# Pair loads and a narrower dense part in a PEER trunk kernel

## The chip, the cores and the metric

The kernel runs on one core of a Trainium2 chip. The metric is the device time of that core for one execution, in microseconds (us). Before the change it was 1577.41 us, the median of three runs (1571.57, 1577.41 and 1578.13).

## The reference, cut to what matters

Two layers act on 256 tokens of width 1024. Each layer mixes tokens (gated convolution, window attention and spatial gating) and then runs PEER: each token picks 16 of 16384 single-neuron experts in each of 8 heads.

```python
q = (t @ w_pq).reshape(T, PEER_HEADS, 2, PEER_HALF)
s = jnp.einsum('thpk,hpnk->thpn', q, sub_keys)
top_s, top_i = lax.top_k(s, PEER_TOPK)            # twice 16 of 128 keys per head
...                                               # best 16 of the 256 sums: experts, gate
u = expert_down[experts]                          # 128 rows of 4 KB for a token
act = gelu(einsum('td,thkd->thk', t, u))
vv = expert_up[experts]                           # 128 more rows
return einsum('thk,thkd->td', gate * act, vv)
```

`expert_down` and `expert_up` are tables of 16384 rows of 1024 float32 numbers, 64 MB each in each layer.

## The kernel before, in words

**Layer 0 and layer 1** have the same stages: mixing, retrieval (queries, key scores, the choice of experts) and experts. The change is about the experts stage, which has two parts of 128 steps each.

**The down part** multiplies the whole down table with the activations: step i takes chunk i of the table (128 experts, 512 KB, one tile `raw` of 128 partitions x 4 KB) and makes 8 products of 128x128 with the first T tokens (line 1233 of `experts`, by `chunk_mm` and line 359). The hidden values go to `acts`, by Gelu and then times a gate matrix that a small matmul makes for four tokens at a time (`gate_mm`, line 1135). **The up part** (`combine`) multiplies the chunks of the up table with `acts`, 8 products for a chunk (line 1173). TensorE is in order, so these chunks set its course.

**The other tokens**, the last S - T, take no part in the dense products, which are T columns wide (`DENSE`, 168 columns in layer 0 and 160 in layer 1). For each of them GpSimd gathers its 128 chosen rows (`fetch`, line 1076: one indirect transfer of 128 rows x 4 KB = 512 KB), first from the down table, where VectorE makes the products (`dot`, line 1086), then from the up table, where VectorE adds them up with weights (`add_row`, line 1101). The sums join the dense result by a few matmuls behind the last chunk (`folds`, line 1179). A gathered row set lies in one of some free places (`free`); a new gather starts when VectorE has used up a place. So layer 0 has 2 x 88 gathers and layer 1 has 2 x 96.

**The order of the loads** is one list, `seq`, for the whole program: conditioning weights, mixing weights and the chunks. Its tiles come from a ring of `RAW` = 7 tiles of 4 KB per partition. Even chunks are issued by ScalarE's queue ("second", line 258, with `QUEUE_LAG`), odd ones by SyncE's (line 217). Fifteen down chunks of a layer ("early") are loaded ahead to places in the arena that nothing else uses yet (`AHEAD_AT`), during mixing and retrieval. Conditioning weights for layer 1 ("aside", 512 KB each) come between the chunks on SyncE's queue; 40 of the 48 come during layer 0's experts stage, and 8 during layer 1's.

**When the gathers start and how fast they are used** follows numbers: `DOT_RATE` sets how many down rows VectorE takes per chunk, and line 1186 spreads the up rows evenly over the chunks from 4 to 124.

Of the kernel before, what the change touches and what calls it, by code (L numbers as in the profile page):

```python
# [9 lines left out]
F32 = mybir.dt.float32  # L10
# [7 lines left out]
P = 128  # L18
DEPTH = 2
S = 256  # L20
DC = 8
D = 1024
# [6 lines left out]

NP = 64  # L30
FRONT = 56
RAW = 7
AHEAD = 300
GROUPS = ("q0", "q1", "kv", "sv", "cc", "ch", "cb", "su")
IN_ORDER = ('q0', 'q1', 'kv', 'sv', 'cc', 'ch', 'cb', 'su')
# [5 lines left out]
PLAN1 = ((5, 'qk_sums k_norm'), (6, 'v_tok'), (7, 'lg10 exp'), (8, 'lg01 lg00 sm00'), (10, 'lg11'), (11, 'sm01 cz'), (12, 'sg'), (13, 'pt00 pt01 sm10 pv0'), (14, 'inv0 ao0 cy pt10'), (15, 'sm11 pt11 inv1 gs4 pv1 as0 ao1 gn4 mix'), (16, 'as1 an0'), (17, 'an1 sqrt'), (20, 'gs6 gn6'))  # L41
G_LAST = 124
OUT_AT = (3, 5, 6, 7)
DENSE = (168, 160)
QUEUE_LAG = 4
PICKS_LAG = 2
LOWER_LAG = 1
# [2 lines left out]
SETS_KNOWN = 22  # L50
D_FIRST = 8
DOT_SLOW = 0.3
DOT_RATE = (0.85, 0.92)
DOT_FAST = 1.6
RETIRE = 9
AHEAD_AT = (8, 12, 16, 36, 40, 44, 48, 52, 56, 60, 64, 68, 100, 28, 32)
KEPT = 100
FLUSH = 6
FIRST_LOWER = 1
AHEAD_FIRST = 4  # L60
# [21 lines left out]

@with_exitstack
def hybrid_trunk(ctx: ExitStack, tc: tile.TileContext, x_in, c_in, vec_in, w_ada, w_in, w_out, w_pq,
                 keys, down, down_rows, up, rel_bias, sgu_w, sgu_b, out):
    nc = tc.nc
    consts = ctx.enter_context(tc.tile_pool(name="consts", bufs=1))
    stream = ctx.enter_context(tc.tile_pool(name="stream", bufs=1))
# [44 lines left out]
    def region(at, *shape):  # L133
        n = 1
        for s in shape:
            n *= s
        v = flat[:, at:at + n]
        if len(shape) == 2:
            v = v.rearrange("p (a b) -> p a b", b=shape[1])
        elif len(shape) == 3:  # L140
            v = v.rearrange("p (a b c) -> p a b c", b=shape[1], c=shape[2])
        return v
# [51 lines left out]
    class Src:  # L194
        credit = 0.0
        loaded = 0
        cast = 0
        seq = []
        later = []
        aside = 0  # L200
# [5 lines left out]
    def dma_ahead(upto):  # L206
        while Src.loaded < min(upto, len(Src.seq)):
            kind, src, raw = Src.seq[Src.loaded]
            if kind == "aside":
                raw = stream.tile([P, D], F32, name="aside", tag=("hi", "lo")[Src.aside % 2], bufs=3)  # L210
                Src.aside += 1
            elif kind != "early":
                raw = stream.tile([P, D], F32, name="raw", tag="raw", bufs=RAW)
            if kind == "second":
                Src.later.append((Src.loaded, raw, src))
            else:
                nc.sync.dma_start(raw, src)
            raws[Src.loaded] = raw
            Src.loaded += 1
# [18 lines left out]
    def ada_end(layer, col, n):  # L238
        if (col + 1) % n == 0:
# [3 lines left out]
            if lo // 8 in (SC1 // 8, SC2 // 8):  # L243
                at = lo % 8 + (V_N1 if lo // 8 == SC1 // 8 else V_N2)
                nc.vector.scalar_tensor_tensor(m, m, 1.0, vec[:, layer, at:at + n], op0=OP.add, op1=OP.mult)

    def load_more(k):
        while Src.loaded < min([len(Src.seq)] + Src.limits) and (Src.ring[Src.loaded + 1] == Src.ring[Src.loaded]
                                             or Src.ring[Src.loaded] <= Src.ring[k + 1] + RAW - 2):
            dma_ahead(Src.loaded + 1)  # L250

    def cast_step(late=None):
        k = Src.cast
        if k >= len(Src.seq):
            return False
        dma_ahead(k + 1)
        while Src.later and Src.ring[Src.later[0][0]] <= Src.ring[k + 1] - 1 + RAW - QUEUE_LAG:
            nc.scalar.dma_start(*Src.later.pop(0)[1:])
        kind, _, arg = Src.seq[k]
        raw = raws.pop(k)  # L260
        Src.cast += 1
        if kind == "aside":
            Src.asides.append((k, lambda: ada_chunk(arg[0], arg[1], raw)))
        elif kind == "ada":
            ada_chunk(arg[0], arg[1], raw)
        elif kind in ("whole", "early", "second"):
            ready.append((raw, None))
        else:
            hi = stream.tile([P, D], F32R, name="hi", tag="hi", bufs=3)
            lo = stream.tile([P, D], F32R, name="lo", tag="lo", bufs=3)  # L270

            def low():
                if arg is None:
                    nc.vector.tensor_sub(lo, raw, hi.bitcast(F32))  # L274
                else:
                    nc.vector.scalar_tensor_tensor(lo, raw, arg, hi.bitcast(F32), op0=OP.mult,
                                                   op1=OP.subtract)

            with tc.high_priority(offset=AHEAD):
                if arg is None:  # L280
                    nc.scalar.copy(hi, raw)  # L281
                else:
                    nc.scalar.activation(hi, raw, AF.Copy, scale=arg)
                if late is None:
                    low()
                else:
                    late.append(low)
            ready.append((hi, lo))
        load_more(k)
        return True  # L290
# [27 lines left out]
    def mats(src, layer, n, kind="mat"):  # L318
        return [(kind, src[layer, p], None) for p in range(n)]

    seq = []
    for layer in range(DEPTH):
        body = [("whole" if n in WHOLE_IN[layer] else "mat", w_in[layer, n], None) for n in range(16)]
        tail = [("whole" if k in WHOLE_OUT[layer] else "mat", w_out[layer, k], vec[:, layer, V_OG + k:V_OG + k + 1])
                for k in OUT_ORDER[layer]]
        if layer == 0:
            first = []
            for d in range(DC):
                first += [("ada", w_ada[0, o + d], (0, o + d)) for o in (SC1, SH1)]
            head = [("early", b[1], region(at * S, 4, S).rearrange("p a b -> p (a b)"))  # L330
                    for b, at in zip(body, EARLY)]
            n = len(head)
            body = head + body[n:]
            body = first[:2] + body[:n] + first[2:] + mix(body[n:], ada(0, [2, 3, 4]))
        body += mix(tail[:6], ada(0, [5])) + tail[6:] if layer == 0 else tail
        seq += body + [("whole" if n in WHOLE_PQ else "mat", w_pq[layer, n], None) for n in range(16)]
        dn, un = ([t if n % 2 else ("second", *t[1:]) for n, t in enumerate(mats(w, layer, 128, "whole"))]
                  for w in (down, up))
        for n, at in enumerate(AHEAD_AT):
            dn[AHEAD_FIRST + n] = ("early", dn[AHEAD_FIRST + n][1], region(at * S, D))  # L340
        aside = ada(1, [0, 1, 2, 3, 4] if layer + 1 < DEPTH else [5], "aside")
        for n, at in reversed(tuple(enumerate(ASIDES_AT[layer]))):
            dn.insert(at, aside[n])
        if layer + 1 < DEPTH:
            un = mix(un, aside[len(ASIDES_AT[layer]):], *ASIDES_UP)
        Src.starts.append(len(seq))
        seq += dn + un
# [2 lines left out]
        Src.ring.append(Src.ring[-1] + was if Src.ring else 0)  # L350
        was = t[0] not in ("early", "aside")
    Src.ring.append(Src.ring[-1] + was)
    dma_ahead(RAW)

    def products(dst, w, cols, k, start, stop, **kw):

# [480 lines left out]
    def retrieval(layer, update, late):  # L837
# [132 lines left out]
        manual.close()  # L970
        for d in range(DC):
            nc.scalar.activation(R_HX[:, d, :], R_H[:, d, :], AF.Identity, bias=shifts[:, d:d + 1])
        Src.limits = [Src.starts[layer] + AHEAD_FIRST + n for n in (10, 13)]
        for pair in range(1, 8):
            if pair > 1:
                ps = bank("ch", 2)
# [33 lines left out]
    def experts(layer, rest):  # L1010
# [151 lines left out]
                a = acts[:, i:i + 2, :tdone]  # L1162
                nc.vector.tensor_mul(a, a, tmp[:, :, :tdone])

        rows = up.rearrange("l j i c -> (l j i) c")

        def combine(layer, late, dotted):
            qg = None
# [60 lines left out]
        for i in range(128):  # L1229
# [66 lines left out]
            n = i - AHEAD_FIRST  # L1296
# [136 lines left out]
```

## Time and profile before

| | |
|---|---|
| median of three runs | 1577.41 us |
| the profiled execution's own time | 1573.99 us |
| its span in the profile | 1572.1 us |
| TensorE busy | 1535.2 us (98%) |
| VectorE busy | 1000.1 us (64%) |
| ScalarE busy | 472.6 us (30%) |
| GpSimd busy | 494.8 us (31%) |
| moved by DMA | 571.21 MB, mean 363 GB/s |

From the times at which the first chunk products and the last ones stand in the trace, the stages of the profiled execution are: mixing and retrieval of layer 0 until 188 us, its down part until 507.5, its up part until 813.3; layer 1's mixing and retrieval until 973.5, its down part until 1283.5 and its up part until 1565.2. A busy TensorE is not a TensorE at its peak, since the ends of matmuls are modelled; how often its matmuls start says more. A row of waits tells which engine at which line waited, for what, how many us in total, how many times, and the longest time. The rows of a DMA view tell a queue's packets, its MB and the share of 16 DMA engines that its packets took; q1 is SyncE's queue, q10 ScalarE's and q0 GpSimd's.

### The profile page before, as it was taken

What the parts mean: (1) busy time and instruction counts of PE and PEld (TensorE: products, weight loads), DVE (VectorE), ACT (ScalarE), POOL (GpSimd) and SP (SyncE); (2) the same over time, 40 slices, a digit from 0 to 9 for tenths busy, and PEclk for the clock granted to TensorE, in tenths of its full rate; (3) what the DMA queues carried; (4) which work ended last, traced back from release to release, by engine and by line L of the source; (5) the groups of instructions that cost most, each with busy time, mean ns of one, the idle gap of its engine ahead of it and who ended that gap; (6) DMA issues with size and microseconds to landing.
All of it is one profiled execution on the core that took longest, in us unless ns stands there. A gap on an engine that the chain in (4) does not pass through costs nothing.

```text
span 1572.1 us, 28958 instructions
## 1 busy us (share of the span) xinstructions
PE 1535.2 (98%) x11240; PEld 1497.3 (95%) x11240; DVE 1000.1 (64%) x2255; ACT 472.6 (30%) x1356; POOL 494.8 (31%) x424
## 2 busy tenths in 40 slices
PE   7999999999999999998999999999999999999998
PEld 5879999999999999998999899999999999999998
DVE  6778898777787454444336678877777764444444
ACT  2346322465554000000025763124665620000000
POOL 1000124433343434444200001244344335445441
PEclk9999999999999999999999999999999999999999
DMA  9998389999999999999964674899999999999997
GB/s 385 343 375 319 134 289 356 418 418 419 418 419 416 417 419 419 418 419 419 419 225 147 202 245 134 289 334 419 418 419 417 419 418 419 419 419 419 419 419 296
DMA packets 156681, 571.21 MB, mean 363 GB/s; under 512 B 18131, under 2 KB 18659, under 8 KB 155392
## 3 DMA queue, kind: packets, MB, share of 16 engines
q1 hardware_dynamic: 66096, 241.07, 39.9%
q0 software_dynamic: 55744, 202.36, 32.2%
q10 hardware_dynamic: 34704, 125.93, 20.0%
q8 instruction: 88, 1.44, 0.3%
q14 instruction: 49, 0.40, 0.1%
HBM read 564.02 MB, written 4.09 MB: 361 GB/s over the span
## 4 chain that ended last, share of the span: by engine, by line
PE 40%; DMA 38%; issue 10%; POOL 5%; DVE 5%; ACT 1%; POOLq 0%; SPq 0%; DVEq 0%; ACTq 0%
DMA arena<-in_up,arena 18%; PE acc L1173 15%; DMA arena<-in_down_rows,arena 14%; PE ch L359 9%; POOL arena L1076 4%; DMA raw<-in_up 4%; PE ch L361 2%; PE ch L362 2%; PE ch L363 2%; PE ch L448 1%; DMA spots<-in_down_rows,arena 1%; DMA raw<-in_w_ada 1%; DVE raw L231 1%; DVE arena L1086 1%; PE g L954 1%
## 5 line engine op out<-in xcount | busy, mean ns | idle before, releaser
L1173 PE MATMUL acc<-arena,raw 128*128 128x168 f32 (+1 forms) x4096 | 574.1, 303 | 11.4 <-DMA raw<-in_up 11.4
L1173 PEld LDWEIGHTS acc<-arena,raw 128*128 128x128 f32 x4096 | 570.4, 190 | 13.6 <-DMA raw<-in_up 13.4
L359 PE MATMUL ch<-arena,raw 128*128 128x168 f32 (+2 forms) x3776 | 560.1, 307 | 0.1
L359 PEld LDWEIGHTS ch<-arena,raw 128*128 128x128 f32 x3776 | 535.6, 190 | 5.8 <-issue 2.0
L1101 DVE SCALAR_TENSOR_TENSOR spots<-arena,spots 128x1024 f32<-128x1024 f32 x156 | 200.4, 1284 | 223.2 <-DMA arena<-in_up,arena 220.8
L1076 POOL DMA_INDIRECT arena<-in_up,arena x159 | 215.7, 1356 | 279.5 <-DMA arena<-in_up,arena 200.1
L1076 POOL DMA_INDIRECT arena<-in_down_rows,arena x151 | 175.8, 1164 | 245.1 <-DVE arena L1086 183.6
L1086 DVE SCALAR_TENSOR_TENSOR arena<-arena,spots 128x1024 f32<-128x1024 f32 x151 | 183.1, 1222 | 82.5 <-DMA arena<-in_down_rows,arena 76.3
L1119 ACT ACTIVATE arena<-arena,parts 128x128 f16<-128x128 f16 x164 | 64.6, 394 | 128.0 <-DVE arena L1109 107.8
L390 ACT ACT_TABLE_LOAD x6 | 7.7, 1283 | 283.2 <-DMA raw<-in_up 283.2
L359 PE MATMUL ch<-arena 128*128 128x160 f32 (+2 forms) x544 | 87.6, 321 | 4.7 <-issue 3.0
L1152 ACT ACTIVATE arena<-ch 128x336 f32<-128x336 f32 (+32 forms) x122 | 42.0, 344 | 164.4 <-PE ch L359 144.0
L359 PEld LDWEIGHTS ch<-arena 128*128 128x128 f32 x544 | 81.4, 195 | 9.8 <-ACT arena L412 4.0
L231 DVE SCALAR_TENSOR_TENSOR aside<-aside,arena 128x1024 f32<-128x1024 f32 x48 | 58.6, 1221 | 42.8 <-DMA aside<-in_w_ada 42.7
L361 PE MATMUL ch<-hh,hi 128*128 128x256 f32 x288 | 82.6, 288 | 2.0 <-DVE arena L479 1.9
L362 PE MATMUL ch<-hh,lo 128*128 128x256 f32 x288 | 81.8, 284 | 0.0
L363 PE MATMUL ch<-hh,hi 128*128 128x256 f32 x288 | 81.8, 284 | 0.0
L274 DVE TENSOR_TENSOR lo<-raw,hi 128x1024 fp32r<-128x1024 f32 x42 | 51.2, 1225 | 33.5 <-ACT hi L281 32.9
L231 DVE SCALAR_TENSOR_TENSOR raw<-raw,arena 128x1024 f32<-128x1024 f32 x48 | 57.9, 1217 | 8.9 <-DMA raw<-in_w_ada 5.3
L1121 ACT ACTIVATE arena<-arena,parts 128x128 f16<-128x128 f16 x164 | 63.5, 387 | 0.0
L1123 ACT ACTIVATE arena<-arena,parts 128x128 f16<-128x128 f16 x164 | 63.5, 387 | 0.0
L1125 ACT ACTIVATE arena<-arena,parts 128x128 f16<-128x128 f16 x164 | 63.4, 387 | 0.0
(231 smaller groups left out, 1662.3 us busy)
## 6 DMA issues: line engine op xcount, KB each, us to landing
raw<-in_up SPq DMA_DIRECT2D x128, 512.0 KB
raw<-in_up ACTq DMA_DIRECT2D x128, 512.0 KB
raw<-in_down SPq DMA_DIRECT2D x114, 512.0 KB
raw<-in_down ACTq DMA_DIRECT2D x112, 512.0 KB
raw<-in_w_ada SPq DMA_DIRECT2D x48, 512.0 KB
aside<-in_w_ada SPq DMA_DIRECT2D x48, 512.0 KB
raw<-in_w_pq SPq DMA_DIRECT2D x32, 512.0 KB
arena<-in_down SPq DMA_DIRECT2D x30, 512.0 KB
```

The lines of the kernel that those rows point to most:

```text
L231: nc.vector.scalar_tensor_tensor(raw, raw, 1.0, cact, op0=OP.mult, op1=OP.mult, accum_out=mods[layer][:, col:col + 1])
L359: nc.tensor.matmul(dst, hi[:, cols], k[0], start=start, stop=stop, **kw)
L361: nc.tensor.matmul(dst, hi[:, cols], k[0], start=start, stop=False, **kw)
L362: nc.tensor.matmul(dst, lo[:, cols], k[0], start=False, stop=False, **kw)
L363: nc.tensor.matmul(dst, hi[:, cols], k[1], start=False, stop=stop, **kw)
L1076: nc.gpsimd.indirect_dma_start(out=held[n], out_offset=None, in_=rows if n >= TS else down_rows[:, :], in_offset=bass.IndirectOffsetOnAxis ...
L1086: nc.vector.scalar_tensor_tensor(row, row, 1.0, R_DX[which(k)[0]], op0=OP.mult, op1=OP.mult, accum_out=R_DOTS[:, k:k + 1])
L1101: nc.vector.scalar_tensor_tensor(R_SUM[s], row, w, R_SUM[s], op0=OP.mult, op1=OP.add)
L1119: nc.scalar.activation(og[0][:, 0, i, :], oh[:, 0, i, :], AF.Copy, scale=parts[:, 0, t + i:t + i + 1])
L1121: nc.scalar.activation(og[1][:, 0, i, :], oh[:, 0, i, :], AF.Copy, scale=parts[:, 1, t + i:t + i + 1])
L1123: nc.scalar.activation(og[0][:, 1, i, :], oh[:, 1, i, :], AF.Copy, scale=parts[:, 0, t + 2 + i:t + 3 + i])
L1173: nc.tensor.matmul(acc[d // 2][:, (d % 2) * S:(d % 2) * S + T], u[:, d * P:(d + 1) * P], acts[:, i, :], start=i == 0 and d % 2 == 0, stop= ...
```

## The change

The host stores the down and up tables so that two neighbouring chunks lie together, 8 KB per partition. One transfer of 1 MB now loads both into one tile of 128 x 2 x 1024. The ring `raw` becomes five such pair tiles (40 KB per partition where it was 28 KB). Loads of other weights use the same ring, two to a tile, and stay 512 KB each. The pairs go in turn by ScalarE's queue and by SyncE's. To make room, the space for GpSimd's descriptors is set to 4096 bytes per partition. The gathers read separate tables in HBM that keep the old layout (for down this was so before; `up_rows` is new).

The dense products of layer 0 become 160 columns wide, as in layer 1. So 96 tokens of layer 0 instead of 88 have their rows gathered, there are 40 groups of gates instead of 42, and `DOT_RATE` of layer 0 is 0.92 as in layer 1. Each early list has 14 chunks instead of 15.

```diff
-RAW = 7
+UNITS = 5
-DENSE = (168, 160)
+DENSE = (160, 160)
-DOT_RATE = (0.85, 0.92)
+DOT_RATE = (0.92, 0.92)
-AHEAD_AT = (8, 12, 16, 36, 40, 44, 48, 52, 56, 60, 64, 68, 100, 28, 32)
+AHEAD_AT = (12, 16, 36, 40, 44, 48, 52, 56, 60, 64, 68, 100, 28, 32)
...
             elif kind != "early":
-                raw = stream.tile([P, D], F32, name="raw", tag="raw", bufs=RAW)
-            if kind == "second":
-                Src.later.append((Src.loaded, raw, src))
+                unit, half = Src.unit[Src.loaded]
+                if half == 0:
+                    Src.open[unit] = stream.tile([P, 2, D], F32, name="raw", tag="raw", bufs=UNITS)
+                raw = Src.open[unit][:, half, :]
+            if kind == "pair":
+                pass
+            elif len(src.shape) == 3 and kind in ("whole", "second"):
+                raw_to = Src.open[unit]
+                if kind == "second":
+                    Src.later.append((Src.loaded, raw_to, src))
+                else:
+                    nc.sync.dma_start(raw_to, src)
             else:
                 nc.sync.dma_start(raw, src)
...
+    def before(n):
+        u = Src.unit[n][0] - UNITS
+        return Src.last[u] if u >= 0 else -1
+
     def load_more(k):
-        while Src.loaded < min([len(Src.seq)] + Src.limits) and (Src.ring[Src.loaded + 1] == Src.ring[Src.loaded]
-                                             or Src.ring[Src.loaded] <= Src.ring[k + 1] + RAW - 2):
+        while Src.loaded < min([len(Src.seq)] + Src.limits) and (
+                Src.unit[Src.loaded] is None or before(Src.loaded) <= Src.ring[k + 1] - 2):
             dma_ahead(Src.loaded + 1)
...
-        dn, un = ([t if n % 2 else ("second", *t[1:]) for n, t in enumerate(mats(w, layer, 128, "whole"))]
-                  for w in (down, up))
+        dn, un = ([("pair", None, None) if n % 2 else ("second" if n % 4 == 0 else "whole", w[layer, n // 2], None)
+                   for n in range(128)] for w in (down, up))
...
-        "down": a["peer_down"].reshape(L, P, P, DC, P).transpose(0, 2, 4, 3, 1).reshape(L, P, P, D),
+        "down": pairs(a["peer_down"].reshape(L, P, P, DC, P).transpose(0, 2, 4, 3, 1).reshape(L, P, P, D)),
-        "up": a["peer_up"].reshape(L, P, P, D).transpose(0, 2, 1, 3),
+        "up": pairs(up_rows),
+        "up_rows": up_rows.reshape(L * P * P, D),
...
-    nc = _bacc.Bacc("TRN2", target_bir_lowering=False, num_devices=1)
+    nc = _bacc.Bacc("TRN2", target_bir_lowering=False, num_devices=1,
+                     dynamic_dma_scratch_size=4096)
```

The first place where the order moves is SyncE's queue at the start of layer 0's down part (`raw` is a ring tile, `aside` a tile for conditioning weights). Before:

```order
L217 DMA aside<-in_w_ada 128x1024 x6
L217 DMA raw<-in_down 128x1024 x13
L217 DMA aside<-in_w_ada 128x1024
L217 DMA raw<-in_down 128x1024 x2
L217 DMA aside<-in_w_ada 128x1024
L217 DMA raw<-in_down 128x1024 x3
```

After the change:

```order
L229 DMA aside<-in_w_ada 128x1024 x6
L227 DMA raw<-in_down 128x2048 x6
L229 DMA aside<-in_w_ada 128x1024
L227 DMA raw<-in_down 128x2048 x2
L229 DMA aside<-in_w_ada 128x1024
L227 DMA raw<-in_down 128x2048
```

Where thirteen and then two or three chunks of 512 KB stood between the asides, six and then one or two pairs stand; the asides keep their places among the chunks.

The second place is GpSimd's queue around the start of layer 0's up part (`spots` and `arena` hold the places of gathered rows). Before, one place in `spots` comes round with nine in `arena`:

```order
L1076 DMA spots<-in_up,arena 128x1024
L1076 DMA arena<-in_up,arena 128x1024 x9
L1076 DMA spots<-in_up,arena 128x1024
L1076 DMA arena<-in_up,arena 128x1024 x5
L533 AFFINE_SELECT arena<-arena 128x512
```

After the change two places in `spots` come round, five gathers apart:

```order
L1104 DMA spots<-in_up_rows,arena 128x1024
L1104 DMA arena<-in_up_rows,arena 128x1024 x5
L1104 DMA spots<-in_up_rows,arena 128x1024
L1104 DMA arena<-in_up_rows,arena 128x1024 x5
L561 AFFINE_SELECT arena<-arena 128x512
```

So layer 0's up part has 12 places for gathered rows where it had 10, as layer 1 has before and after.

More of the change, by code (lines that the diff above doesn't have):

```diff
@@ L84, in hybrid_trunk @@
 def hybrid_trunk(ctx: ExitStack, tc: tile.TileContext, x_in, c_in, vec_in, w_ada, w_in, w_out, w_pq,
-                 keys, down, down_rows, up, rel_bias, sgu_w, sgu_b, out):
+                 keys, down, down_rows, up, up_rows, rel_bias, sgu_w, sgu_b, out):
     nc = tc.nc
@@ L197, in hybrid_trunk @@
         cast = 0
+        unit = []
+        last = []
+        open = {}
         seq = []
@@ L256, in cast_step @@
         dma_ahead(k + 1)
-        while Src.later and Src.ring[Src.later[0][0]] <= Src.ring[k + 1] - 1 + RAW - QUEUE_LAG:
+        while Src.later and before(Src.later[0][0]) <= Src.ring[k + 1] - 1 - QUEUE_LAG:
             nc.scalar.dma_start(*Src.later.pop(0)[1:])
@@ L265, in cast_step @@
             ada_chunk(arg[0], arg[1], raw)
-        elif kind in ("whole", "early", "second"):
+        elif kind in ("whole", "early", "second", "pair"):
             ready.append((raw, None))
@@ L336, in hybrid_trunk @@
         seq += body + [("whole" if n in WHOLE_PQ else "mat", w_pq[layer, n], None) for n in range(16)]
-        dn, un = ([t if n % 2 else ("second", *t[1:]) for n, t in enumerate(mats(w, layer, 128, "whole"))]
-                  for w in (down, up))
+        dn, un = ([("pair", None, None) if n % 2 else ("second" if n % 4 == 0 else "whole", w[layer, n // 2], None)
+                   for n in range(128)] for w in (down, up))
         for n, at in enumerate(AHEAD_AT):
-            dn[AHEAD_FIRST + n] = ("early", dn[AHEAD_FIRST + n][1], region(at * S, D))
+            c = AHEAD_FIRST + n
+            dn[c] = ("early", down[layer, c // 2, :, c % 2, :], region(at * S, D))
         aside = ada(1, [0, 1, 2, 3, 4] if layer + 1 < DEPTH else [5], "aside")
@@ L352, in hybrid_trunk @@
     Src.ring.append(Src.ring[-1] + was)
-    dma_ahead(RAW)
+    for n, t in enumerate(seq):
+        if t[0] in ("early", "aside"):
+            Src.unit.append(None)
+            continue
+        fresh = not Src.last or len(filled) == 2 or (t[0] in ("second", "whole") and len(t[1].shape) == 3)
+        if fresh:
+            filled = []
+            Src.last.append(None)
+        Src.unit.append((len(Src.last) - 1, len(filled)))
+        filled.append(n)
+        Src.last[-1] = Src.ring[n]
+    dma_ahead(2 * UNITS)
     def products(dst, w, cols, k, start, stop, **kw):
@@ L972, in retrieval @@
             nc.scalar.activation(R_HX[:, d, :], R_H[:, d, :], AF.Identity, bias=shifts[:, d:d + 1])
-        Src.limits = [Src.starts[layer] + AHEAD_FIRST + n for n in (10, 13)]
+        Src.limits = [Src.starts[layer] + AHEAD_FIRST + n for n in (9, 12)]
         for pair in range(1, 8):
@@ L1163, in act_use @@
                 nc.vector.tensor_mul(a, a, tmp[:, :, :tdone])
-        rows = up.rearrange("l j i c -> (l j i) c")
+        rows = up_rows[:, :]
         def combine(layer, late, dotted):
@@ L1404, with pairs @@
     sb = np.broadcast_to(sb, (L, 2, 2, 64, P)).transpose(0, 2, 3, 1, 4).reshape(L, P, 2, P)
+    def pairs(w):
+        return w.reshape(L, P // 2, 2, P, D).transpose(0, 1, 3, 2, 4)
+    up_rows = a["peer_up"].reshape(L, P, P, D).transpose(0, 2, 1, 3)
     arrays = {
```

## The prediction

> **What bounds the kernel now.** I read the page first, for its totals and its 40 slices.
>
> ```profile
> span 1572.1 us, 28958 instructions
> PE 1535.2 (98%) x11240; PEld 1497.3 (95%) x11240; DVE 1000.1 (64%) x2255; ACT 472.6 (30%) x1356; POOL 494.8 (31%) x424
> PEclk9999999999999999999999999999999999999999
> GB/s 385 343 375 319 134 289 356 418 418 419 418 419 416 417 419 419 418 419 419 419 225 147 202 245 134 289 334 419 418 419 417 419 418 419 419 419 419 419 419 296
> ```
>
> Two things are full at once: TensorE, at a granted clock that never falls, and the DMA, which stands at 418 or 419 GB/s through two long plateaus. The stretches between the stage limits say where (engines' busy us, then clock, DMA share and GB/s):
>
> ```profile
> 0.00:188.00 188.00, 173.93 (x1080) 155.02 (x1081) 144.95 (x412) 81.64 (x173) 9.99 (x19) 1.00 0.85 319
> 188.00:255.00 67.00, 65.75 (x463) 64.86 (x462) 60.78 (x305) 14.84 (x28) 27.00 (x32) 1.00 0.82 271
> 255.00:507.50 252.50, 252.26 (x1950) 249.59 (x1950) 184.63 (x353) 134.16 (x474) 94.67 (x79) 1.00 1.03 418
> 507.50:787.00 279.50, 269.56 (x1879) 267.64 (x1878) 128.97 (x126) 0.45 (x1) 110.18 (x84) 1.00 1.03 419
> 787.00:813.30 26.30, 26.30 (x191) 26.30 (x190) 6.61 (x8) 4.28 (x7) 0.00 (x0) 1.00 0.81 275
> 973.50:1045.00 71.50, 69.65 (x502) 69.24 (x501) 65.10 (x314) 15.20 (x29) 26.73 (x28) 0.98 0.81 271
> 1045.00:1283.50 238.50, 236.19 (x1891) 232.44 (x1891) 168.50 (x320) 126.50 (x453) 96.26 (x88) 1.00 1.03 418
> 1283.50:1545.00 261.50, 260.02 (x1915) 259.78 (x1914) 112.99 (x92) 0.72 (x2) 124.05 (x89) 1.00 1.03 419
> 1545.00:1572.00 27.00, 22.41 (x170) 22.16 (x168) 15.06 (x17) 0.00 (x0) 1.43 (x1) 0.97 0.60 242
> ```
>
> Layer 0's DMA is full from 255 to 787 us and layer 1's from 1045 to 1545. Which of the two full things sets the end? The waits of the up parts, layer 0 first (507.5 to 813.3 us), then layer 1:
>
> ```profile
> PE acc L1173 <- DMA raw<-in_up: 9.9, 6, 3.4
> ...
> PE acc L1173 <- DMA raw<-in_up: 1.5, 1, 1.5
> DVE spots L1101 <- DMA arena<-in_up,arena: 126.9, 74, 3.5
> ```
>
> TensorE waits for chunks 9.9 us in layer 0 and 1.5 us in layer 1. VectorE waits for gathered rows all through, 126.9 us in layer 1, so the gathers take whatever the chunks leave of the bus. What remains is whether they come in before TensorE is done. VectorE's rows near the end of each layer, layer 0 first:
>
> ```profile
> 795.71 1.28 DVE L1101 SCALAR_TENSOR_TENSOR spots<-arena,spots 128x1024 f32<-128x1024 f32 x1 [1.73 <-DMA arena<-in_up,arena]
> ...
> 1555.31 7.89 DVE L1101 SCALAR_TENSOR_TENSOR spots<-arena,spots 128x1024 f32<-128x1024 f32 x6 [1.41 <-DMA arena<-in_up,arena]
> ```
>
> Layer 0's last gathered row is added at 795.7, 17.6 us before its up part ends at 813.3. In layer 1 six rows are still to be added at 1555.3, 9.9 us before the end at 1565.2. So layer 1 is in balance, and layer 0 has a little bus to spare and loses a little to a burst. The change narrows TensorE's work in layer 0 and gives the bus more to carry.
>
> **TensorE.** Starts of its passes in the up part (two passes make one product), 168 columns wide in the first row and 160 in the second:
>
> ```profile
> 510.00:640.00 130.00, 130.00 (x915) 130.00 (x914) 1.00 1.03 418
> ...
> 1300.00:1500.00 200.00, 200.00 (x1475) 200.00 (x1474) 1.00 1.03 419
> ```
>
> 130/915 is 142.1 ns for a pass and 200/1475 is 135.6 ns. Layer 0 has 2 x 128 x 16 = 4096 such passes, so its dense work shrinks by 4096 x 6.5 ns = 26.6 us. That is a gain only where the bus keeps up.
>
> **The bus, more bytes.** A gather moves 128 x 4 KB = 0.524 MB, at 419 GB/s 1.251 us. Sixteen more of them in layer 0 (eight down, eight up) cost 16 x 1.251 = +20.0 us of a full bus. On VectorE and GpSimd, by the page's groups:
>
> ```profile
> L1101 DVE SCALAR_TENSOR_TENSOR spots<-arena,spots 128x1024 f32<-128x1024 f32 x156 | 200.4, 1284 | 223.2 <-DMA arena<-in_up,arena 220.8
> L1076 POOL DMA_INDIRECT arena<-in_up,arena x159 | 215.7, 1356 | 279.5 <-DMA arena<-in_up,arena 200.1
> ...
> L1086 DVE SCALAR_TENSOR_TENSOR arena<-arena,spots 128x1024 f32<-128x1024 f32 x151 | 183.1, 1222 | 82.5 <-DMA arena<-in_down_rows,arena 76.3
> ```
>
> On VectorE they are 8 x 1.22 + 8 x 1.28 = 20 us, covered, since it is busy 184.6 of 252.5 us and 129.0 of 279.5; without the cover they would be 20 us too. GpSimd's 16 issues of 1.36 us lie in its idle time (94.7 busy of 252.5); uncovered, they would be another 22.
>
> **The bus, larger packets.** The trace of before has packets of 8 KB: the load of x at the start, alone on the bus. Its row, and behind it one of 4 KB packets alone:
>
> ```profile
> DMA packets 91, 0.64 MB, mean 426 GB/s; under 512 B 7, under 2 KB 13, under 8 KB 14
> q1 hardware_dynamic: 81, 0.63, 101.4%
> ...
> DMA packets 2307, 8.40 MB, mean 420 GB/s; under 512 B 256, under 2 KB 256, under 8 KB 2307
> ```
>
> 426 against 420 GB/s makes 0.0176 us for 0.524 MB. How many chunks move on the plateaus, by the issues between 255 and 813 us:
>
> ```profile
> raw<-in_up SPq DMA_DIRECT2D x64, 512.0 KB
> raw<-in_up ACTq DMA_DIRECT2D x64, 512.0 KB
> raw<-in_down SPq DMA_DIRECT2D x47, 512.0 KB
> raw<-in_down ACTq DMA_DIRECT2D x47, 512.0 KB
> ...
> raw<-in_w_in SPq DMA_DIRECT2D x7, 512.0 KB
> ```
>
> 222 x 0.0176 = -3.9 us in layer 0, and about the same in layer 1. Below, it may be nothing, since the stretch of 8 KB packets is short (1.5 us); above, 426 against the plateau's 418 makes -5.2 us. I take -3.9, since both its rows have one queue alone. The Trainium skill, in "DMA: Bandwidth & Descriptors", section "Why small descriptors are slow (HBM only)", gives each packet a fixed cost of some 3 cycles beside one cycle for 32 bytes. As an estimate from it, 8 KB would take 259 cycles where two of 4 KB take 262, 1.1% less, and the term would be -3.1 us; the row shows 1.4%.
>
> **The bus, an earlier start.** Loads that move ahead of 255 us, where the bus runs at 271 GB/s, leave the plateau. The ring holds ten chunks where it held seven, one early chunk is gone: two more. Two more places for gathers: two more. TensorE, faster by 6.5 ns a pass, is about one chunk further at 255. That is five times 1.251, or -6.3 us, with nothing as the other end, if those loads only come later in the gaps; I take -4, nearer the full value, because right before the down part the bus stands still and the ring can be filled there:
>
> ```profile
> 176.00:188.00 12.00, 12.00 (x104) 12.00 (x103) 9.56 (x54) 2.94 (x5) 2.42 (x3) 1.00 0.00 1
> ```
>
> **Layer 0, the sum.** From 787 to 813.3 the bus moved 26.3 x 275 = 7.2 MB, of which 3.7 MB are the seven loads of the next layer's weights in the row above. With a full bus the rest would have been in at 787 + 3.56/0.419 = 795.5 us. Now +20.0 - 3.9 - 4 gives 807.6. Behind the last row stand the last adds and the closing matmuls, 9.9 us in layer 1: 817.5 at the latest, against 813.3; the last six adds need not all stand behind the last row, and one chunk (16 x 0.136 = 2.2 us) and the closing matmuls certainly do, so about 812. I take the middle, 815: **+1.5 us**, in place of TensorE's -26.6. A second way to it: layer 1 is layer 0 as it will be, but for the asides,
>
> ```profile
> L231 DVE SCALAR_TENSOR_TENSOR aside<-aside,arena 128x1024 f32<-128x1024 f32 x40 | 48.9, 1222 | 42.8 <-DMA aside<-in_w_ada 42.7
> ...
> L231 DVE SCALAR_TENSOR_TENSOR aside<-aside,arena 128x1024 f32<-128x1024 f32 x8 | 9.7, 1218 | 0.0
> ```
>
> 32 of which are 32 x 1.251 = 40.0 us of bus. Its experts stage takes 1565.2 - 973.5 = 591.7 us; 591.7 + 40.0 - 3.9 - 2.5 (two chunks of the ring) = 625.3, against 625.0 for layer 0 now. Both ways say: no change in layer 0.
>
> **Layer 1.** The bus is relieved by 3.9 + 2.5 = 6.4 us, but TensorE is as full as before, and what it visibly waits for a chunk in the up part is 1.5 us. Between 0 and -6.4 I take **-3**.
>
> **Elsewhere.** Mixing and retrieval load the same 512 KB tiles from a deeper ring. VectorE's wait there for conditioning weights bounds the gain:
>
> ```profile
> DVE raw L231 <- DMA raw<-in_w_ada: 5.3, 3, 2.0
> ```
>
> Between 0 and -5.3, I take **-1**, since at the start the bus is full anyway. A pair is usable only when both halves have landed, 1.25 us later for the first half; the ring's five pairs cover it, and without that cover it would be 1.25 us once at each refill. Behind a pair that waits for its tile stand SyncE's asides and next pairs; VectorE waits for asides (42.7 us in layer 0) without TensorE waiting for it in the up part. Two groups of gates fewer in layer 0 are under 1 us. The smaller descriptor space shows in no row; a gather's flight does, in the chain of waits of layer 1's up part:
>
> ```profile
> 1478.99 22.83 DMA arena<-in_up,arena
> ```
>
> Its cost is zero if the flights still fit (22.8 us each, at 96 gathers in 281.6 us, so eight at a time), and at most tens of us if GpSimd has to wait for a landing before it can issue; nearest is layer 1, whose number of places does not change, and I take zero.
>
> **Sum:** +1.5 - 3 - 1 = -2.5 us. The profiled execution took 1573.99 us, 3.4 below the median of the runs shown; -2.5 from it is 1571.5 and from the median 1574.9. I forecast **1573 us**, no change that can be told (a measurement here tells about 0.5%, 7.9 us: 1569.5 to 1585.3 is "same"). Its own range is 1562 to 1582.
>
> **Rivals.**
> - *The columns decide.* If the bus has more to spare than its plateau shows, because the gathers only ran ahead of need, layer 0 falls towards layer 1's 591.7 us: up to -33.3 - 4, or 1537; half of it gives 1555. For it: rows done 17.6 us ahead of the end, and TensorE's 9.9 us in six waits that a deeper ring rides out. Against it: 20 us of bytes on a bus at 418.
> - *The gathers become the end of layer 0.* TensorE finishes its narrower chunks early, the ring's ten tiles come free and SyncE fills them with the next layer's weights, in front of the last gathers: 10 x 1.251 = 12.5 us, and the earlier start brings nothing (+4): 1573 + 16.5 = 1589. It decides once the last row of layer 0 is added after its last chunk's products. For it: `QUEUE_LAG` and the pacing let the chunks run ahead. Against it: the next layer's weights are needed then anyway.
> - *Turns on the bus.* The chunk queues' packets double, the gathers' do not. If each queue in turn sends one packet, a gather that had 4 of 12 KB in a round has 4 of 20 KB whenever both chunk queues are backlogged; in the down parts VectorE then waits for rows, the gates queued behind them on VectorE come late, and TensorE waits. One refill of 5 MB ahead of the rows is 12.5 us of bus; at one of the two down parts: 1585, at both 1598. The Trainium skill, "DMA: Bandwidth & Descriptors", section "Queues, rings and completion order", says that an engine goes round the queues by packets. No row here shows packets of unequal size in competition for long.
> - *The pairs do nothing:* packets as fast or cut to 4 KB. The terms -3.9 and -3 go: 1580. Against it: the load of x did show 8 KB packets.
>
> **How the numbers follow.** Chances: forecast 0.50 (faster 0.17, same 0.32, slower 0.01), columns 0.20 (faster), gathers at the end 0.16 (same 0.03, slower 0.13), turns 0.08 (same 0.02, slower 0.06, a GpSimd short of descriptors among them), pairs nothing 0.06 (same 0.05, slower 0.01). So faster 0.37, same 0.42, slower 0.21. The range goes from 1552, which leaves out the far half of the first rival, to 1592, which leaves out the worst of the second and third.
>
> **What would show it.** Right: layer 0's passes at 135.6 ns with waits on `raw<-in_up` growing to 20 us or more, its plateau at 421 to 423 GB/s until its last rows, which are added within some 10 us of the end; layer 1 within 591.7 and 585. Wrong: a plateau that ends long before the stage does (columns decide), a plateau still at 419 (pairs nothing), last rows added well after the last chunk's product (gathers), or, together with waits of TensorE on gates, more waits of VectorE for down rows than this of layer 0 now (turns):
>
> ```profile
> DVE arena L1086 <- DMA arena<-in_down_rows,arena: 37.7, 39, 2.4
> ```

## The result, and the profile after

The changed kernel takes 1592.71 us (median of four runs, 1591.01 to 1593.13), the kernel before 1577.77 beside it: a ratio of 1.0103, with a 95% interval of 1.0085 to 1.0120. It is 1% slower. The profiled execution took 1591.01 us, 17.0 more than that of before.

The page of the changed kernel, for its totals and slices:

```profile
span 1589.3 us, 28428 instructions
PE 1518.2 (96%) x11208; PEld 1477.9 (93%) x11208; DVE 1015.9 (64%) x2273; ACT 470.9 (30%) x1338; POOL 533.5 (34%) x437
...
PEclk9999999999999999999969999999999999999999
...
GB/s 386 364 383 301 100 322 348 422 422 420 422 422 410 423 423 423 422 424 423 421 283 160 158 240 121 281 349 415 419 422 423 419 423 422 423 424 423 422 424 244
...
q10 hardware_dynamic: 17424, 125.93, 19.1%
```

TensorE is 17.0 us less busy than before, and the span is 17.2 us longer. The plateaus stand mostly at 420 to 424 GB/s instead of 416 to 419, so the pairs do what they say: ScalarE's queue moves its 125.93 MB in half as many packets (34704 before). One slice shows a granted clock of 6 tenths. The stretches of the changed kernel show where (busy us and instructions of PE, PEld, DVE, ACT and POOL; clock, DMA share, GB/s):

```profile
255.00:520.00 265.00, 253.46 (x1924) 242.74 (x1924) 191.61 (x366) 127.92 (x456) 108.67 (x92) 0.98 1.02 417
520.00:797.40 277.40, 277.40 (x2044) 277.40 (x2043) 115.31 (x112) 4.11 (x5) 105.62 (x75) 1.00 1.02 423
797.40:833.00 35.60, 3.99 (x19) 3.85 (x18) 30.70 (x29) 1.25 (x4) 16.25 (x15) 0.57 0.73 284
...
1064.00:1302.60 238.60, 235.87 (x1881) 233.40 (x1880) 169.07 (x324) 130.73 (x453) 115.21 (x90) 0.99 1.02 420
1302.60:1562.00 259.40, 259.40 (x1911) 259.40 (x1911) 111.10 (x88) 0.44 (x1) 121.00 (x87) 1.00 1.02 423
```

The first three rows are layer 0's down part, its up part and its end; the last two are layer 1's down and up parts. In layer 0's up part TensorE runs without a gap until 797.4 us and then does next to nothing for 32 us, in the middle of its last chunk. TensorE's timeline there, and VectorE's:

```profile
797.43 0.33 PE L1207 MATMUL acc<-fold,spots 128*128 128x64 f32 x2
829.37 0.64 PE L1207 MATMUL acc<-fold,spots 128*128 128x32 f32 x2 [31.61 <-DVE qg L565]
```

```profile
805.33 1.28 DVE L1129 SCALAR_TENSOR_TENSOR spots<-spots,arena 128x1024 f32<-128x1024 f32 x1
806.64 6.57 DVE L1129 SCALAR_TENSOR_TENSOR spots<-arena,spots 128x1024 f32<-128x1024 f32 x5
813.25 1.28 DVE L1129 SCALAR_TENSOR_TENSOR spots<-spots,arena 128x1024 f32<-128x1024 f32 x1
814.57 6.82 DVE L1129 SCALAR_TENSOR_TENSOR spots<-arena,spots 128x1024 f32<-128x1024 f32 x5
821.42 1.28 DVE L1129 SCALAR_TENSOR_TENSOR spots<-spots,arena 128x1024 f32<-128x1024 f32 x1
822.75 6.57 DVE L1129 SCALAR_TENSOR_TENSOR spots<-arena,spots 128x1024 f32<-128x1024 f32 x5
```

Line 1207 is `folds`, which needs the sums of all gathered rows. The waits name VectorE's next instruction behind the adds (line 565). When TensorE has finished its chunks, 21 of the 96 up rows are still to be added. Up to 805 us VectorE waits for each; from then on each row is there in time and it adds 17 of them one behind the other, about 1.31 us each, until 829.

Stage by stage, from the first down chunk's product to the last product of an up chunk (us):

| | before | after | predicted |
|---|---|---|---|
| until layer 0's down part | 188.3 | 189.6 | |
| layer 0, down part | 319.3 | 330.5 | |
| layer 0, up part | 305.7 | 312.9 | |
| layer 0, both | 625.0 | 643.4, +18.4 | +1.5 |
| mixing and retrieval, layer 1 | 160.2 | 159.3 | |
| layer 1, both | 591.7 | 589.7, -2.0 | -3 |
| after the last chunk | 6.9 | 7.3 | |

These times, and those of layer 0 below, come from one profiled execution of each kernel, while the whole times of one kernel scatter by 1 to 11 us between runs. So differences of a few us between stage times are worth less than ratios of whole kernels.

### The profile page after: what moved, and what is told of

Read it like the earlier page. It is cut to its first block, busy times and chain, and to the rows that moved or that the text cites. A ratio compares the mean times of both kernels' runs of the same rounds, so it can differ in the third digit from the quotient of the medians.

```text
span 1589.3 us, 28428 instructions
## 1 busy us (share of the span) xinstructions
PE 1518.2 (96%) x11208; PEld 1477.9 (93%) x11208; DVE 1015.9 (64%) x2273; ACT 470.9 (30%) x1338; POOL 533.5 (34%) x437
## 3 DMA queue, kind: packets, MB, share of 16 engines
q1 hardware_dynamic: 48528, 241.06, 38.3%
q10 hardware_dynamic: 17424, 125.93, 19.1%
## 4 chain that ended last, share of the span: by engine, by line
PE 53%; DMA 34%; DVE 7%; issue 3%; ACT 1%; POOL 1%; SPq 0%; DVEq 0%; POOLq 0%; ACTq 0%
PE ch L387 19%; DMA arena<-in_up_rows,arena 18%; PE acc L1201 18%; DMA arena<-in_down_rows,arena 14%; PE ch L389 2%; PE ch L390 2%; PE ch L391 2%; DVE spots L1129 1%; PE g L1163 1%; DMA raw<-in_w_ada 1%; POOL arena L1104 1%; PE ch L476 1%; DVE arena L1114 1%; PE g L982 1%; PE acc L391 1%
## 5 line engine op out<-in xcount | busy, mean ns | idle before, releaser
L387 PE MATMUL ch<-arena,raw 128*128 128x160 f32 (+1 forms) x3808 | 560.3, 306 | 4.4 <-issue 3.9
L1201 PE MATMUL acc<-arena,raw 128*128 128x160 f32 x4096 | 559.3, 299 | 0.0
L1104 POOL DMA_INDIRECT arena<-in_up_rows,arena x160 | 219.2, 1370 | 287.5 <-DMA arena<-in_up_rows,arena 200.4
L1147 ACT ACTIVATE arena<-arena,parts 128x128 f16<-128x128 f16 x160 | 63.3, 395 | 139.4 <-DVE arena L1137 128.3
L387 PE MATMUL ch<-arena 128*128 128x160 f32 (+1 forms) x512 | 79.4, 315 | 1.6 <-ACT arena L440 1.4
L1180 ACT ACTIVATE arena<-ch 128x320 f32<-128x320 f32 (+30 forms) x122 | 41.8, 343 | 123.0 <-PE ch L387 97.5
L1163 PE MATMUL g<-arena 128*128 128x128 f16 x640 | 60.3, 221 | 13.9 <-ACT arena L1147 11.9
L1104 POOL DMA_INDIRECT spots<-in_down_rows,arena x42 | 48.5, 1156 | 71.5 <-DVE spots L1114 44.9
L1173 DVE SCALAR_TENSOR_TENSOR arena<-arena,g 128x248 f32<-128x248 f32 (+29 forms) x80 | 39.4, 492 | 51.3 <-ACT arena L1171 49.6
L1163 PEld LDWEIGHTS <-arena 128*128 128x128 f16 x640 | 45.1, 96 | 26.4 <-ACT arena L1147 15.3
```

Of the source, the lines that this page charges most:

```text
L387: nc.tensor.matmul(dst, hi[:, cols], k[0], start=start, stop=stop, **kw)
L1104: nc.gpsimd.indirect_dma_start(out=held[n], out_offset=None, in_=rows if n >= TS else down_rows[:, :], in_offset=bass.IndirectOffsetOnAxis ...
L1147: nc.scalar.activation(og[0][:, 0, i, :], oh[:, 0, i, :], AF.Copy, scale=parts[:, 0, t + i:t + i + 1])
L1163: nc.tensor.matmul(dst, og[j][:, i // 2, i % 2, :], on[:, i // 2, :, i % 2], start=j == 0, stop=j == 1)
L1180: nc.scalar.activation(acts[:, i:i + 2, tdone:], v[:, :, tdone:T], AF.Gelu)
L1201: nc.tensor.matmul(acc[d // 2][:, (d % 2) * S:(d % 2) * S + T], u[:, d * P:(d + 1) * P], acts[:, i, :], start=i == 0 and d % 2 == 0, stop= ...
```

## The experiments

All ratios are to the kernel before, run beside the kernels on the same chip, with 95% intervals. Layer 0's time is that of its experts stage, as in the table.

**Pairs with 168 columns.** One half of the change alone.

```diff
-DENSE = (160, 160)
+DENSE = (168, 160)
...
-DOT_RATE = (0.92, 0.92)
+DOT_RATE = (0.85, 0.92)
```

> The pairs and their ring with layer 0's dense products 168 columns wide again (88 gathered tokens, DOT_RATE 0.85). Theory A (the columns did it: 16 more gathers come in after TensorE's narrower chunks, and the pairs are harmless or good): 1568 to 1575 us, no wait of TensorE for layer 0's last rows above 5 us, layer 0's plateau at 421 to 424 GB/s. Theory B (the pairs did it: larger packets and a deeper ring starve the gathers): 1583 us or more, with a wait of 10 us or more for the last rows of layer 0.

Measured: 1565.15 us against 1573.00, ratio 0.9945 (0.9929 to 0.9961), 3 us below the range of theory A. Layer 0 takes 616.9 us, 8.1 less than before, and TensorE's only wait in its up part is this:

```profile
PE acc L1207 <- DVE qg L565: 0.9, 1, 0.9
```

So the columns did it, as theory A had it, and the pairs without them are a gain. This version beats both kernels.

**Single chunks with 160 columns.** The other half alone, on the kernel before.

```diff
-DENSE = (168, 160)
+DENSE = (160, 160)
...
-DOT_RATE = (0.85, 0.92)
+DOT_RATE = (0.92, 0.92)
```

> The kernel before with layer 0's dense products 160 columns wide (DOT_RATE 0.92), single chunks and a ring of seven. Theory A: 1594 to 1602 us, that is the changed kernel without the 4 to 8 us that faster packets save; TensorE either waits for the last rows of layer 0 or for chunks on the way. Theory B: 1580 us or less, since nothing starves the gathers.

Measured: 1596.28 us, ratio 1.0151 (1.0134 to 1.0168). Layer 0 takes 643.3 us, 18.3 more than before and as long as with pairs, but TensorE waits elsewhere:

```profile
PE acc L1173 <- DMA raw<-in_up: 15.6, 15, 2.8
PE acc L1179 <- DVE qg L537: 8.2, 1, 8.2
```

Sixteen rows are 16 x 1.251 = 20.0 us of bus; 18.3 of them show. By these two executions the bus of layer 0 had 1.7 us to spare.

**Packets of 4 KB in the ring of pairs,** at 160 columns.

```diff
-                if kind == "second":
-                    Src.later.append((Src.loaded, raw_to, src))
-                else:
-                    nc.sync.dma_start(raw_to, src)
+                for h in range(2):
+                    if kind == "second":
+                        Src.later.append((Src.loaded, raw_to[:, h, :], src[:, h, :]))
+                    else:
+                        nc.sync.dma_start(raw_to[:, h, :], src[:, h, :])
```

> The changed kernel with each pair loaded by two transfers of 512 KB on the same queue, one behind the other, so that packets are 4 KB as before while the ring, the columns and the order stay. Theory A: slower than the changed kernel by what the packets save, 4 to 8 us in all, 1596 to 1601; plateau at 419 GB/s. Theory B in its form with turns (8 KB packets against the gathers' 4 KB): faster than the changed kernel, 1585 or less, with a shorter wait of TensorE for layer 0's last rows than 31.6 us.

Measured: 1598.78 us, ratio 1.0159 (1.0134 to 1.0185). Layer 0 takes 650.8 us, 7.4 more than with whole pairs. TensorE's waits in the up part:

```profile
PE acc L1208 <- DVE qg L566: 15.0, 1, 15.0
PE acc L1202 <- DMA raw<-in_up: 12.5, 8, 5.8
```

With whole pairs it waits 31.6 us for the last rows and never for chunks. The same 260 us of the up part, 530 to 790, first with halves and then with whole pairs:

```profile
DMA packets 29753, 108.89 MB, mean 419 GB/s; under 512 B 3299, under 2 KB 3427, under 8 KB 29494
...
q0 software_dynamic: 10904, 39.71, 37.4%
```

```profile
DMA packets 21610, 109.92 MB, mean 423 GB/s; under 512 B 2398, under 2 KB 2526, under 8 KB 13858
...
q0 software_dynamic: 9816, 35.76, 33.7%
```

With larger packets for the chunks GpSimd's queue gets 35.76 MB instead of 39.71, 7.5 rows fewer, so this part of theory B's form with turns is seen. But the bytes that the rows lose go to the chunks and, with whole pairs, to five early loads of layer 1's weights; TensorE waits at the end instead of on the way, and the total is better. So the turns decide who waits, and no loss by them shows here.

**Layer 1's weights behind the gathers,** at 160 columns.

```diff
...
-                nc.sync.dma_start(raw, src)
+                q = nc.gpsimd if Src.win <= Src.loaded < Src.win + 10 else nc.sync
+                q.dma_start(raw, src)
...
+        if layer == 0:
+            Src.win = len(seq)
```

(`Src.win` is the place of layer 1's first mixing weight in the list of loads.)

> The changed kernel with the first ten loads of layer 1's mixing weights issued from GpSimd's queue, so behind the last gathers of layer 0 instead of in front of them on SyncE's queue. If those loads hold up the last gathers, as my second rival had it (ten of 1.25 us): 1580 to 1585 us and a wait of TensorE of 20 to 25 us. If the gathers are late for the chunks alone and these loads only use what is left: 1589 to 1595, or slower because layer 1's weights come later.

Measured: 1585.66 us, ratio 1.0078 (1.0061 to 1.0095), just above the first expectation and below the second. TensorE's wait at the end falls from 31.6 to 25.9 us,

```profile
PE acc L1211 <- DVE spots L1133: 25.9, 1, 25.9
```

and layer 0 takes 637.5, 5.9 less. So the weights do stand in front of the last rows, and that is worth some 6 of the 12.5 us that the second rival gave; most of the lateness is not theirs. Over the whole kernel the interval overlaps that of the changed kernel (1.0085 to 1.0120), so the gain is not shown beyond doubt.

**The same with 168 columns,**

> Pairs with layer 0 at 168 columns, and the first ten loads of layer 1's mixing weights behind the gathers on GpSimd's queue. In the 168 run the last rows came in time (0.9 us of wait), so there is nothing to gain: equal to that run (ratio to before 0.993 to 0.997), or up to 3 us slower since the weights come later. If it is faster by over 3 us, the weights in front of the gathers cost something there too.

gives 1567.93 us, ratio 0.9949 (0.9925 to 0.9973): nothing to gain where the rows come in time. Layer 0 took 622.6 us in its profiled execution, 5.7 more than in that of the pairs with 168 columns, though the ratios agree.

**Less on the bus.** The changed kernel without the 18 loads of conditioning weights in layer 0's up part.

```diff
-            else:
+            elif kind != "aside" or not 22 < Src.aside <= 40:
                 nc.sync.dma_start(raw, src)
...
-        nc.vector.scalar_tensor_tensor(raw, raw, 1.0, cact, op0=OP.mult, op1=OP.mult,
+        skip = layer == 1 and 22 <= col < 40
+        nc.vector.scalar_tensor_tensor(raw, cact if skip else raw, 1.0, cact, op0=OP.mult, op1=OP.mult,
```

> The changed kernel without the 18 loads of conditioning weights in layer 0's up part (VectorE still runs its 18 operations, on other data; so a part of layer 1's modulation is not computed from its weights). If layer 0 is bound by the bytes of the bus: 18 x 1.24 = 22 us of bus go, TensorE's wait for the last rows falls from 31.6 to 8 to 12 us, and the time falls by 18 to 22 us against the changed kernel, to about before minus 4. If the end is bound by VectorE's adds and the flights of the last rows, not by bytes: the wait stays above 20 us and the gain is under 10.

This kernel leaves out that part of layer 1's modulation; VectorE's 18 operations are still there, on other data. Measured: 1562.57 us, ratio 0.9906 (0.9873 to 0.9938). Layer 0 takes 620.5 us, 22.9 less than the changed kernel; that is 1.27 us for each load of 0.524 MB. The profiled execution was the slowest of the four (1557.53 to 1567.18 us): the median fell by 30.1 us, more than the 18 to 22 expected, and what the rest is stays open. The wait at the end:

```profile
PE acc L1208 <- DVE qg L566: 8.1, 1, 8.1
```

In the changed kernel's up part VectorE had no wait for a conditioning weight, so it is not such waits that went. Layer 0 at 160 columns is bound by the bytes of the bus, and not by VectorE's adds or by the flights of the last rows.

**A ring of four pairs,** at 160 columns (`UNITS = 4`).

> The changed kernel with a ring of four pairs (eight chunks). Theory C (chunks run ahead, take the bus first and leave the gathers a tail in which the bus is not full and VectorE adds row after row): 4 to 8 us faster than the changed kernel, with a shorter wait at the end than 31.6 us and a few us of waits for chunks instead. Theory A (bytes alone, however they are ordered): equal to the changed kernel within 3 us.

Measured: 1602.47 us, ratio 1.0178 (1.0153 to 1.0203). Theory C falls. The rows now come in time, the last is added 15 us before the last chunk's product, but TensorE waits for chunks instead, in layer 0 and also in layer 1, whose up part takes 293.7 us instead of 279.4. The waits of layer 0's up part:

```profile
PE acc L1201 <- DMA raw<-in_up: 25.9, 15, 2.6
```

Layer 0 takes 640.6 us, 2.8 less than with five pairs: the same within 3 us, however the waits are spread. The loss in layer 1 neither expectation foresaw. GpSimd's queue, in the 260 us from 530 to 790, with the large packets beside it as before:

```profile
q0 software_dynamic: 11973, 43.59, 41.0%
```

That is more than with 4 KB packets in a ring of five pairs (39.71 MB). So the packets' size alone does not set the gathers' share; how far the ring lets the chunks run ahead counts as well.

**Fewer down rows in the down part,** at 160 columns (`DOT_RATE` 0.85 in layer 0).

> The changed kernel with DOT_RATE 0.85 in layer 0, so that fewer down rows are multiplied in its down part and more are left to its up part. If bytes bind the whole stage: the down part gets some 5 us shorter and the up part as much longer, the sum equal to the changed kernel within 3 us. If the down part pays for the rate itself (VectorE's products hold up the gates): 5 us or more faster in all.

Measured: 1593.86 us, ratio 1.0119 (1.0097 to 1.0141). The down part takes 322.4 us and the up part 322.2, with a wait of 38.3 us at its end; together 644.6 against 643.4. The down part got 8.1 us shorter and the up part 9.3 longer, and the sum stayed, as expected for bytes that bind the whole stage; so the 11.2 us by which the change made the down part longer go with the rows that it moves.

**What gives the gain at 168 columns?** Three kernels: the kernel before with the smaller descriptor space alone, the same with a ring of ten single chunks (`RAW = 10`), and the pairs at 168 columns with halves as above.

> The kernel before with 4096 bytes per partition for GpSimd's descriptors and nothing else. If the space does not matter, as the prediction took it: ratio to before 0.998 to 1.002. If GpSimd has to wait for room: slower by over 0.5%, with longer waits of GpSimd before its gathers.

> The kernel before (168 columns, single chunks of 512 KB) with a ring of ten tiles in place of seven, and the 4096 bytes that make room for it. If the 8 us that pairs at 168 columns gained in layer 0 come from the depth of the ring, which rides out the burst in which TensorE waited 9.9 us for chunks: 0.994 to 0.997 of before, without those waits. If they come from the packets: 0.998 to 1.004.

> Pairs with layer 0 at 168 columns, each pair loaded by two transfers of 512 KB, so packets of 4 KB in the same ring. If the gain at 168 columns is the ring's: 0.994 to 0.997 of before, as with whole pairs. If it is the packets': 0.999 to 1.006, that is 6 to 14 us slower than whole pairs, as at 160 columns.

Measured, in this order: 1.0014 (1.0000 to 1.0028), 0.9951 (0.9935 to 0.9968) and 1.0006 (0.9991 to 1.0020). The descriptor space costs nothing that can be told from the runs' scatter. The deeper ring alone gives what whole pairs give (0.9945); TensorE's chunk waits in layer 0's up part shrink from 9.9 us to 3.9, and layer 0 takes 621.0 us:

```profile
PE acc L1173 <- DMA raw<-in_up: 3.9, 1, 3.9
```

But the same depth in pairs with 4 KB packets gives nothing, with 4.7 us of chunk waits and layer 0 at 623.1. So loading pairs by halves loses something that whole pairs do not lose.

**The deeper ring at 160 columns.** The ring of ten single chunks, to look for that loss.

```diff
-RAW = 7
+RAW = 10
...
-DENSE = (168, 160)
+DENSE = (160, 160)
...
-DOT_RATE = (0.85, 0.92)
+DOT_RATE = (0.92, 0.92)
...
-    nc = _bacc.Bacc("TRN2", target_bir_lowering=False, num_devices=1)
+    nc = _bacc.Bacc("TRN2", target_bir_lowering=False, num_devices=1,
+                     dynamic_dma_scratch_size=4096)
```

> The kernel before with a ring of ten single chunks, the 4096 bytes that make room for it, and layer 0 at 160 columns (DOT_RATE 0.92). From its first down chunk to its last up chunk layer 0 took 643.3 us with seven single chunks at 160 columns, and 650.8 with five pairs of 4 KB packets. If the deeper ring costs where rows come last (more of layer 1's weights in front of them): layer 0 takes 647 to 652 us, ratio to before 1.014 to 1.019. If the 7.5 us between those two were the pairs' own (two issues at a time on ScalarE's queue): layer 0 takes 640 to 645, ratio 1.008 to 1.014.

Measured: 1592.34 us, ratio 1.0115 (1.0098 to 1.0132), layer 0 at 646.1 us, between the two expectations. The 2.8 us more than with seven single chunks (643.3) are no price of the depth: the first down product comes 2.0 us earlier (186.3 us instead of 188.3), the last up product only 0.8 us later, and over the whole kernel the deeper ring is the faster of the two (1.0115 against 1.0151). Pairs loaded by halves, a ring as deep, are slower than ten single chunks (1.0159). TensorE's wait for the first products' evacuation by ScalarE, with halves and then with the ten single chunks:

```profile
PE ch L388 <- ACT arena L1181: 4.1, 1, 4.1
```

```profile
PE ch L359 <- ACT arena L1152: 2.7, 1, 2.7
```

In both, ScalarE's instruction follows right behind loads issued on its own queue (two in 3.83 us, three in 2.82); in the changed kernel a single load of 0.33 us stands there, and this wait is missing. That these loads cause the wait fits, but no run shows it by itself. It is 1.4 us longer with halves; what the rest of their loss is stays open. Whole pairs and ten single chunks cannot be told apart, at 160 columns (1.0103 and 1.0115) or at 168 (0.9945 and 0.9951).

## Why the prediction was wrong, point by point

**TensorE's columns.** Predicted 135.6 ns for a pass at 160 columns. Right; the up part of layer 0:

```profile
600.00:797.00 197.00, 197.00 (x1452) 197.00 (x1451) 1.00 1.02 422
```

197/1452 is 135.7 ns. And right that the narrower columns are no gain: nothing of the 26.6 us arrives. (That the clock of before never falls was read from tenths; the prediction's own rows have 0.97 and 0.98 in layer 1. Nothing rests on it.)

**More bytes.** Right, at its size: 20.0 us predicted for sixteen rows, 18.3 measured with single chunks, and 1.27 us for each conditioning load that was left out, by the profiled execution, where I took 1.251 for a gather of the same size.

**Larger packets.** The direction is right, the size not settled: -3.9 us in layer 0 predicted. Between halves and whole pairs it is -7.4 at 160 columns and -6.2 at 168, but halves are also two issues; between ten single chunks and whole pairs, where the ring is as deep, it is -2.7 and -4.1. On the plateau itself 419 becomes 423 GB/s (108.89 and 109.92 MB in 260 us). Of the latter 57 pairs, 59.8 MB, go in 8 KB packets: 0.95% over 0.54 of the bytes is 1.8% for those, where the load of x had shown 1.4%. The Trainium skill's 3 cycles for a packet ("DMA: Bandwidth & Descriptors", "Why small descriptors are slow (HBM only)") had given 1.1% as an estimate; the direction agrees, the measurement is larger.

**The earlier start.** Wrong: -4 us predicted. What had moved by 255 us, before and after:

```profile
DMA packets 21288, 78.11 MB, mean 306 GB/s; under 512 B 2642, under 2 KB 2786, under 8 KB 20753
```

```profile
DMA packets 20160, 78.57 MB, mean 308 GB/s; under 512 B 2675, under 2 KB 2803, under 8 KB 18359
```

That is 0.46 MB, 1.1 us. I counted the ring's depth as filled while the bus stood still, but it stood still in the changed kernel too (1 GB/s from 176 to 189.6 us): the kernel's own limits on the loads (`Src.limits`) hold then, and ScalarE's queue issues nothing between 163 and 203 us. Two more chunks had been issued by 255 us, but two gathers fewer.

**Layer 0, the sum: the step that failed.** +1.5 us predicted, +18.4 measured. The step is the room that I credited on the bus. I let the bus of before be done at 795.5 us, by taking what it moved after 787 at full rate, and put 7.4 us behind the last row. So I credited 813.3 - 795.5 - 7.4 = 10.4 us that layer 0 had to spare, and with it, the packets and the early start paid for the sixteen rows. The single chunks at 160 columns show 1.7 us to spare. The sign that I had given, waits for chunks of 20 us or more, did not come: the up part has none, and TensorE's wait of 31.6 us is for the last rows.

The row on which it rested, the last add of before at 795.71, was read too generously. A bus below its plateau at the end of the stage need not be room for the loads before it: such a stretch stands at the end of the changed kernel's layer 0 as well. From 797.4 to 833.0 us it moved 284 GB/s, so 35.6 x (1 - 284/423) = 11.7 us of it went unused, where before it was 26.3 x (1 - 275/419) = 9.0. And until 787 the bus of before was full while TensorE waited 9.9 us for chunks.

Split by the runs with single chunks, the +18.4 are +18.3 (sixteen rows), +2.8 (ring of ten, most of it the stage's earlier start) and -2.7 (whole pairs in place of ten single chunks). These are differences of neighbouring runs, so they add up by construction; only the first is clearly larger than the runs' scatter.

The second way, layer 0 as layer 1 with 32 more asides, gave 625.3. It left out other loads of layer 0. What the experts stages of the changed kernel moved, layer 0 (189.6 to 833 us) and then layer 1 (992.3 to 1582 us):

```profile
DMA packets 53732, 257.05 MB, mean 400 GB/s; under 512 B 6408, under 2 KB 6536, under 8 KB 38192
```

```profile
DMA packets 47539, 234.63 MB, mean 398 GB/s; under 512 B 5720, under 2 KB 5720, under 8 KB 32128
```

Layer 0 moves 22.4 MB more, 53.0 us at 423 GB/s, and takes 643.4 - 589.7 = 53.7 us longer. Of the 22.4 MB the 32 asides are 16.8. The rest are eight loads of layer 1's first weights (4.2 MB) and the tables for layer 1's mixing (1.4 MB), 13 us that the second way did not count. It also took 6.4 us off for the pairs and the ring, where layer 1 itself got 2.0 us shorter.

**Layer 1 and elsewhere.** -3 predicted, -2.0 measured in the profiled executions; -1 predicted for mixing and the rest, +0.8 measured in the first stage, layer 1's mixing and the last stage (1.3 - 0.9 + 0.4). Right within what one execution tells.

**The rivals.** What happened is the second one in place and time: the last rows of layer 0 come after the last chunk, 1589 predicted, 1592.7 measured. That its time came so near is in part luck: layer 1's weights in front of the rows explain 5.9 us where it took 12.5, and the bytes of the stage the rest. "The columns decide" is refuted by the single chunks at 160 columns, 18.3 us longer in layer 0, and by the wait for the last rows, 0.9 us with pairs at 168 columns and 31.6 at 160. "Turns" are seen (7.5 rows fewer in 260 us), without a loss by them. Its other sign came too, TensorE waiting for gates in layer 0's down part, which it did not do before: the first row is the changed kernel's, the second that of single chunks with 4 KB packets.

```profile
PE g L1163 <- ACT arena L1147: 9.3, 13, 2.0
```

```profile
PE g L1135 <- ACT arena L1119: 10.7, 13, 3.9
```

So these waits come with layer 0's 160 columns and not with the packets. "The pairs do nothing" is refuted by the plateau, 423 GB/s, and by the halves. The range ended at 1592, 0.7 below the time, because it left out the far end of the second rival and the likeliest case rested on the spare bus.

## What to carry to other kernels

Where two resources are full at once, a shift of work from one to the other is paid for in full by the other: here 16 transfers at 1.25 us each, of which 18.3 us arrived, while TensorE's waits in layer 0 grew from 11.1 us to 43.2, by more than the 26.6 us taken off its work. Do not read spare room out of an early last arrival while the transfer rate stands at its plateau; run the shift alone, or drop some transfers, and see the price. When one stage is forecast from another, compare the bytes that both move, and not one kind of load. A deeper ring is worth its space where it rides out a burst (0.5% here, without any larger packets), and two edits bundled in one change are best run apart: one of these gains 0.55% and the other loses 1.5%.

## What the runs showed of the hardware

Packets of 8 KB beside packets of 4 KB on the same DMA engines raised the plateau from 419 to 423 GB/s and moved 3.7 points of the engines' share from the queue with the small packets to those with the large (37.4% to 33.7%); with a shallower ring and the same large packets the small ones had 41.0%.

TensorE was idle for 32 us at the end of layer 0, and its granted clock fell to 0.50 there, after 1.00 in the stretch before:

```profile
805.00:823.00 18.00, 0.00 (x0) 0.00 (x0) 17.47 (x18) 0.00 (x0) 11.96 (x12) 0.50 0.97 369
```

The closing matmuls right behind it took 4.32 us for twenty, where the same twenty at the end of layer 1 took 2.31:

```profile
833.27 4.32 PE L1207 MATMUL acc<-fold,spots 128*128 128x64 f32 x20
...
1582.10 2.31 PE L1207 MATMUL acc<-fold,spots 128*128 128x64 f32 x20
```

The mixing that followed took no longer for it (159.3 us against 160.2).
